# A hybrid decoder layer on one core: two of the weights' four sums by adding transfers, and more chunks with seven products

## The chip, the cores and the metric

One core of a Trainium2 chip. The time is the device time of one launch in microseconds (us). Before the change, three runs took 2104.35, 2105.90 and 2107.91 us; the median is 2105.9.

## What is computed

One decoder layer with 256 tokens, a width of 2048 and a feed-forward width of 5632, all in float32:

```python
def swiglu(x, w_gate, w_up, w_down):
    return (jax.nn.silu(x @ w_gate) * (x @ w_up)) @ w_down

h = h + 0.5 * swiglu(rmsnorm(h, g_ffn1), w1_gate, w1_up, w1_down)
z = rmsnorm(h, g_mix) @ w_in                 # gating MLP and window attention
h = h + concat(rmsnorm(y_a), rmsnorm(y_b)) @ w_out
h = h + cross_attention(rmsnorm(h, g_x), rmsnorm(mem, g_mem), w_xq, w_xkv, w_xo)
h = h + 0.5 * swiglu(rmsnorm(h, g_ffn2), w2_gate, w2_up, w2_down)
out = rmsnorm(h, g_final)
```

The two feed-forwards hold most of the work: two matrices of 2048 x 5632 and one of 5632 x 2048 each.

## The kernel before, in words

**Chunks and units.** Every weight matrix is streamed once, in chunks of 256 rows by two blocks of 512 columns: a tile of [128, 4, 512] float32, 1 MB, whose four rows are called B12, B11, B22 and B21 (slots 0 to 3). A *unit* is all the chunks that add up to the same output columns. In the gate and up part of a feed-forward a unit has 8 chunks (one block of 512 columns of the gate, one of up), and there are 11 units. The down part has 22 chunks and two halves of columns; they are run in four units of 8, 15, 15 and 7 chunks.

**Three matmuls for one product.** A float32 product is made of three passes in fp32r: each operand is split into a high part (a cast, ACT, L148) and a low part (source minus high part, DVE, L149), and high x high, low x high and high x low are summed in PSUM.

**Seven products for eight.** The activations of a chunk are also four blocks (two blocks of 128 tokens by two of 128 rows). A chunk of kind N or C does the 8 block products, 24 matmuls. A chunk of kind S does Strassen's seven (Winograd's form), 21 matmuls; for that it needs four sums of weights, T1 = B11 + B12, T3 = B12 + B22, T2 = T1 + B22 and T4 = T2 + B21, and these have to be split as well. The string KINDS gives the kinds of a unit's 8 chunks, KINDS_D those of the 22 chunks of the down part. C is a kind with 24 matmuls whose activation blocks are combined so that its results fall into the same banks as those of S.

**Loads.** `load` (L298) issues the transfer of a chunk on SP's queue, the split on ACT and DVE, and for S the sums on DVE (L310 two rows at once, L313, L314). There are three buffers for raw chunks, two for high and for low parts, one for the sums (t) and one each for their high and low parts (th, tl). So the transfer of chunk n can start when chunk n-3 has been read by its split and its sums, and chunk n can be split when the matmuls of n-2 have gone through.

**Banks.** PSUM has two pools of four banks. P2, Q3, Q5 and Q4 lie in one (acc). P1, Q7 and Q6, which only S chunks write, lie in the other (trp), from the first S chunk of a unit to the one at index 6; transposes and other side work use what is left of it.

**The end of a unit.** `seven_early` (L479, after chunk 6) copies P1 on ACT and makes v = Q6 - P1 and z = Q7 + v on DVE. `seven_late` (L487, after chunk 7) adds P2, Q5 (twice), Q4 and Q3 to these, which frees the acc banks for the next unit; SiLU on ACT and a product (L585) follow. The 128 x 512 activations so made are transposed on PE (`rows_done`, L565), in two groups of four, a few matmuls into the next unit, and copied by ACT (L575).

**What sets the order.** PE runs in the order of the program. The other engines' instructions, and the transfers that SP and POOL issue, are put in order by a scheduler from priorities and its own costs when the program is built; on the chip each engine takes its own in that order. Chunk 0 and the last chunk of a unit do their products bank by bank (`by_bank`, L349); the others keep the low parts that come last to the end of the chunk.

Of the kernel before, what the change touches and what calls it, by code (L numbers as in the profile page):

```python
# [25 lines left out]
G_FFN1, G_MIX, G_X, G_MEM, G_FFN2, G_Y, B_S = 0, 16, 32, 48, 64, 80, 96  # L26
# [4 lines left out]
def layer_kernel(  # L31
# [22 lines left out]
    nc = tc.nc  # L54
# [3 lines left out]
    stream = ctx.enter_context(tc.tile_pool(name="stream", bufs=2))  # L58
# [9 lines left out]
    def nm(s):  # L68
        uid[0] += 1
        return f"{s}_{uid[0]}"  # L70
# [76 lines left out]
    def split(hi, lo, src):  # L147
        nc.scalar.copy(hi, src)  # L148
        nc.vector.tensor_tensor(lo, src, hi.bitcast(F32), ALU.subtract)  # L149
# [17 lines left out]
    shared = []  # L167
# [84 lines left out]
    def pair_normalized(s, kind, srcT, i, gcol, by_token):  # L252

        raw = s2(s + "r").rearrange("p (k t) -> p k t", k=4)
        src = srcT[i * T:(i + 1) * T, :].rearrange("(k p) t -> p k t", p=P)
        for tb in range(TB):
            a, b = laid(kind, 0, tb), laid(kind, 1, tb)
            nc.gpsimd.dma_start(raw[:, a:b + 1:b - a, :], src[:, :, tb * P:(tb + 1) * P])
        turned = 1 if kind == "S" else 0
        for k in range(2):  # L260
            c = gcol + 2 * i + k
            o = row_tile(kind, raw, k)
            nc.vector.scalar_tensor_tensor(
                out=o, in0=o, scalar=sm[:, c:c + 1], in1=by_token[:, turned:turned + 2, :],
                op0=ALU.mult, op1=ALU.mult,
            )
        p = Pair(s, kind)
        fill(s, p, raw)
        return p
# [28 lines left out]
    def load(s, w, kind, pieces):  # L298

        raw = stream.tile([P, 4, 512], F32, tag="raw", name=nm(s + "w"), bufs=3)  # L300
        wh = stream.tile([P, 4, 512], F32R, tag="wh", name=nm(s + "wh"))
        wl = stream.tile([P, 4, 512], F32R, tag="wl", name=nm(s + "wl"))
        b = {name: (wh[:, i, :], wl[:, i, :]) for name, i in SLOT.items()}
        if kind == "S":
            nc.sync.dma_start(raw, w)
            t = stream.tile([P, 4, 512], F32, tag="t", name=nm(s + "t"), bufs=1)
            th = stream.tile([P, 4, 512], F32R, tag="th", name=nm(s + "th"), bufs=1)
            tl = stream.tile([P, 4, 512], F32R, tag="tl", name=nm(s + "tl"), bufs=1)
            split(wh[:, 1:, :], wl[:, 1:, :], raw[:, 1:, :])
            nc.vector.tensor_tensor(  # L310
                t[:, 0:2, :], raw[:, 1:3, :], raw[:, 0:1, :].to_broadcast([P, 2, 512]), ALU.add
            )
            nc.vector.tensor_tensor(t[:, 2, :], t[:, 0, :], raw[:, 2, :], ALU.add)  # L313
            nc.vector.tensor_tensor(t[:, 3, :], t[:, 2, :], raw[:, 3, :], ALU.add)  # L314
            split(th, tl, t)
            for i, name in enumerate(("T1", "T3", "T2", "T4")):
                b[name] = th[:, i, :], tl[:, i, :]
        elif pieces:
            for i in pieces:
                nc.sync.dma_start(raw[:, i, :], w[:, i, :])  # L320
                split(wh[:, i, :], wl[:, i, :], raw[:, i, :])
        else:
            nc.sync.dma_start(raw, w)
            split(wh, wl, raw)
        return b
# [50 lines left out]
    def side_add(gen):  # L376
        side.append([now[0], gen])
# [62 lines left out]
    def unit(s, w, cb, pairs, beside=None):  # L440

        u = Unit(s, "N" * 8)
        for i in range(8):
            if beside is not None:
                beside(i)
            push(u, i, w[i, cb], lambda i=i: have(pairs, i))
        flush()
        return {(tb, j): u[name] for name, tb, j in BLOCKS}
# [31 lines left out]

# [80 lines left out]
    def ffn(s, get, rs, wgu, wd, on_block, first=None):  # L561
# [36 lines left out]
        def gu_unit(c):  # L598
# [10 lines left out]

            u = Unit(s + "g", KINDS)  # L610
            for i in range(8):
# [159 lines left out]
    n2, on2, rs2_ = next_norm("n2", G_MIX)  # L771
# [2 lines left out]
        first=(n0, prep1, lambda: rs1[0]),  # L774
    )
    mT = []
    partsm = tiny.tile([P, TB, NG], F32, tag="parts", name=nm("parts"))

    def mem_squares(j):
# [34 lines left out]
    by_token = const.tile([P, 3, P], F32, name="by_token")  # L814
# [151 lines left out]
    pu = unit("u", w_in, 0, n2, lambda i: mT.append(pair_normalized("mT", KINDS[i], memT, i, G_MEM, by_token)))  # L966
    with tc.high_priority():
        for name, tb, j in BLOCKS:
            nc.scalar.activation(
# [181 lines left out]
    for cb in range(2):  # L1151
        both = rows_scaled("xq", unit("xq", w_xq, cb, n3), rs3_())
        for j in range(2):
            side_add(attend_memory(2 * cb + j, both[j]))

    n4, on4, rs4_ = next_norm("n4", G_FFN2, KINDS)
    for cb in range(2):
        added_unit("xo", w_xo, cb, xo, on4)
# [114 lines left out]
```

## Time and profile before

| | |
|---|---|
| median of three runs | 2105.9 us |
| profiled execution, and its span | 2105.79 us, 2104.0 us |
| mean granted clock of PE | 0.996 |
| PE, DVE, ACT, POOL busy | 2076.0, 1674.5, 1135.4, 32.2 us |
| read from HBM | 398.52 MB |
| SP's queue q1 | 393.50 MB, 51.7% of 16 engines |
| POOL's queue q0 | 6.30 MB, 0.9% |

A row of a timeline gives start and length in us, engine, line of the kernel, operation, out<-in, and in brackets how long the engine had been idle and what it waited for. A row of a group gives line, engine, operation, shapes and count, then busy time and the mean in ns of one, then idle time of the engine before them and what ended it. In the names, f1g and f2g are the gate and up parts of the two feed-forwards, f1d and f2d the down parts; w, wh, wl are raw chunk, high and low part, t, th, tl the same of the sums; f1gP and f1gQ are the banks.

### The profile page before, as it was taken

Reading aid. Unit: us, or ns where it says so; the run is one execution under the profiler, and the core shown is the slowest. Engines: PE = TensorE matmul, PEld = TensorE weight load, DVE = VectorE, ACT = ScalarE, POOL = GpSimd, SP = SyncE. Lnnn points to the kernel's source line nnn. Section 1 sums busy time; section 2 is a strip of 40 time slices with the busy share of each in tenths; the row PEclk is TensorE's granted clock in tenths of the full one; section 3 lists DMA queues with packets and bytes.
Section 4 is the critical chain, followed back from the end, with each engine's and each line's share of the span. In section 5 each row is a group of like instructions: output and inputs, shape, how many; then the busy total and the mean of one; then the engine's idle time right before and its main releaser. Section 6 shows DMA issues by size and latency. Waiting matters only on the chain.

```text
span 2104.0 us, 23815 instructions
## 1 busy us (share of the span) xinstructions
PE 2076.0 (99%) x9527; PEld 1715.5 (82%) x9527; DVE 1674.5 (80%) x1609; ACT 1135.4 (54%) x1109; POOL 32.2 (2%) x51
## 2 busy tenths in 40 slices
PE   9999999999999999999999999999999999999998
PEld 7888888888888888788888888778888888888886
DVE  5888888888987745867858657798888888889878
ACT  7655555555544645544545455665555545555444
POOL 0000000000000000100000000000000000000000
PEclk9999999999999999999999999999999999999999
DMA  7555555555555554435555543455555555555553
GB/s 281 195 189 213 200 195 184 209 188 199 202 199 206 201 210 166 167 140 200 180 180 184 197 160 140 163 197 200 181 207 197 204 191 200 200 200 200 200 198 122
DMA packets 60110, 402.15 MB, mean 191 GB/s; under 512 B 6864, under 2 KB 8928, under 8 KB 12768
## 3 DMA queue, kind: packets, MB, share of 16 engines
q1 hardware_dynamic: 57280, 393.50, 51.7%
q0 software_dynamic: 2016, 6.30, 0.9%
q8 instruction: 74, 1.21, 0.2%
q10 hardware_dynamic: 704, 0.84, 0.1%
q14 instruction: 36, 0.29, 0.0%
HBM read 398.52 MB, written 2.10 MB: 190 GB/s over the span
## 4 chain that ended last, share of the span: by engine, by line
PE 94%; DVE 3%; ACT 1%; issue 1%; DMA 1%; POOL 0%; SPq 0%; POOLq 0%; DVEq 0%; ACTq 0%
PE f2gQ L363 16%; PE f1gQ L363 15%; PE f1dQ L363 6%; PE f2dQ L363 6%; PE f2gP L363 6%; PE f1gP L363 5%; PE f1dP L363 3%; PE f2dP L363 3%; PE woQ L363 2%; PE xqQ L363 2%; PE f1dR L363 2%; PE f2dR L363 2%; PE xoQ L363 2%; PE mk0Q L363 1%; PE mv1Q L363 1%; PE mv0Q L363 1%
## 5 line engine op out<-in xcount | busy, mean ns | idle before, releaser
L149 DVE TENSOR_TENSOR f1gwl<-f1gw,f1gwh 128x2048 fp32r<-128x2048 f32 (+1 forms) x91 | 185.5, 2043 | 51.6 <-ACT f1gwh L148 51.4
L148 ACT CAST f2gwh<-f2gw 128x1536 fp32r<-128x1536 f32 (+1 forms) x88 | 154.4, 1755 | 133.4 <-PE f2gQ L363 96.6
L148 ACT CAST f1gwh<-f1gw 128x2048 fp32r<-128x2048 f32 (+1 forms) x91 | 156.1, 1716 | 123.5 <-PE f1gQ L363 90.4
L149 DVE TENSOR_TENSOR f2gwl<-f2gw,f2gwh 128x1536 fp32r<-128x1536 f32 (+1 forms) x88 | 183.7, 2088 | 40.3 <-ACT f2gwh L148 40.2
L363 PE MATMUL f2gQ<-f2gwh,n4fh 128*128 128x512 f32 x363 | 141.4, 390 | 0.0
L363 PE MATMUL f2gQ<-f2gwh,n4fl 128*128 128x512 f32 x363 | 141.3, 389 | 0.0
L363 PE MATMUL f1gQ<-f1gwh,n1fh 128*128 128x512 f32 x330 | 128.6, 390 | 0.0
L363 PE MATMUL f1gQ<-f1gwh,n1fl 128*128 128x512 f32 x330 | 128.4, 389 | 0.0
L148 ACT CAST f2dwh<-f2dw 128x2048 fp32r<-128x2048 f32 (+1 forms) x44 | 79.2, 1799 | 91.2 <-PE f2dQ L363 71.2
L148 ACT CAST f1dwh<-f1dw 128x2048 fp32r<-128x2048 f32 (+1 forms) x44 | 79.2, 1799 | 87.9 <-PE f1dQ L363 68.2
L149 DVE TENSOR_TENSOR f2dwl<-f2dw,f2dwh 128x2048 fp32r<-128x2048 f32 (+1 forms) x44 | 94.4, 2145 | 27.0 <-ACT f2dwh L148 24.3
L363 PE MATMUL f2gQ<-f2gwl,n4fh 128*128 128x512 f32 x363 | 115.7, 392 | 0.0
L149 DVE TENSOR_TENSOR f1dwl<-f1dw,f1dwh 128x2048 fp32r<-128x2048 f32 (+1 forms) x44 | 94.3, 2144 | 26.8 <-ACT f1dwh L148 24.2
L363 PE MATMUL f1gQ<-f1gwl,n1fh 128*128 128x512 f32 x330 | 105.1, 392 | 0.0
L149 DVE TENSOR_TENSOR f2gtl<-f2gt,f2gth 128x2048 fp32r<-128x2048 f32 x33 | 75.6, 2292 | 17.0 <-ACT f2gth L148 16.6
L149 DVE TENSOR_TENSOR f1gtl<-f1gt,f1gth 128x2048 fp32r<-128x2048 f32 x30 | 68.8, 2292 | 18.3 <-ACT f1gth L148 18.0
L363 PEld LDWEIGHTS f2gQ<-f2gwh,n4fl 128*128 128x128 f32 x363 | 68.1, 188 | 14.2
L363 PEld LDWEIGHTS f2gQ<-f2gwh,n4fh 128*128 128x128 f32 x363 | 68.2, 188 | 14.1
L363 PEld LDWEIGHTS f2gQ<-f2gwl,n4fh 128*128 128x128 f32 x363 | 67.3, 188 | 13.5
L148 ACT CAST f2gth<-f2gt 128x2048 fp32r<-128x2048 f32 x33 | 63.1, 1913 | 23.1 <-DVE f2gt L314 18.3
L363 PEld LDWEIGHTS f1gQ<-f1gwh,n1fl 128*128 128x128 f32 x330 | 62.0, 188 | 12.9
L363 PEld LDWEIGHTS f1gQ<-f1gwh,n1fh 128*128 128x128 f32 x330 | 62.0, 188 | 12.8
(703 smaller groups left out, 5715.1 us busy)
## 6 DMA issues: line engine op xcount, KB each, us to landing
f2gw<-in_w_gu SPq DMA_DIRECT2D x88, 1024.0 KB, 4.8
f1gw<-in_w_gu SPq DMA_DIRECT2D x87, 1024.0 KB, 4.8
f1dw<-in_w_down SPq DMA_DIRECT2D x44, 1024.0 KB, 4.8
f2dw<-in_w_down SPq DMA_DIRECT2D x44, 1024.0 KB, 4.8
wow<-in_w_out SPq DMA_DIRECT2D x16, 1024.0 KB, 4.8
xqw<-in_w_xq SPq DMA_DIRECT2D x16, 1024.0 KB, 4.8
xow<-in_w_xo SPq DMA_DIRECT2D x16, 1024.0 KB, 4.8
qw<-in_w_in SPq DMA_DIRECT2D x8, 1024.0 KB, 5.0
```

Source lines behind the costliest of these rows:

```text
L148: nc.scalar.copy(hi, src)
L149: nc.vector.tensor_tensor(lo, src, hi.bitcast(F32), ALU.subtract)
L363: nc.tensor.matmul(self.banks[name], x, y, start=name not in self.begun, stop=self.left[name] == 0)
```

## The change

1. `KINDS` goes from CCSCSCSC to SCSCSCSC for the gate and up parts: four of eight chunks are S. The memory's keys and values keep the old string as `KINDS_M`.
2. `KINDS_D` has 8 S in 22 chunks; it had 6.
3. In an S chunk T1 and B12 + B22 are no longer made by DVE. SP loads B11 into slot 0 of the raw tile, B22 into row 0 of t, and slots 1 to 3 as before; POOL then issues two transfers that add B12 to slot 0 (which becomes T1) and to t's row 0 (T3). DVE makes T2 and T4. One split covers all four slots of the raw tile, one the three rows of t. B12 by itself is no longer kept. This holds for all S chunks, in the other stages too. The tile t has three rows and two buffers.
4. `shared.clear()` in two places drops a half-used buffer for the sums of C chunks.

```diff
         if kind == "S":
-            nc.sync.dma_start(raw, w)
-            t = stream.tile([P, 4, 512], F32, tag="t", name=nm(s + "t"), bufs=1)
-            th = stream.tile([P, 4, 512], F32R, tag="th", name=nm(s + "th"), bufs=1)
-            tl = stream.tile([P, 4, 512], F32R, tag="tl", name=nm(s + "tl"), bufs=1)
-            split(wh[:, 1:, :], wl[:, 1:, :], raw[:, 1:, :])
-            nc.vector.tensor_tensor(
-                t[:, 0:2, :], raw[:, 1:3, :], raw[:, 0:1, :].to_broadcast([P, 2, 512]), ALU.add
-            )
-            nc.vector.tensor_tensor(t[:, 2, :], t[:, 0, :], raw[:, 2, :], ALU.add)
-            nc.vector.tensor_tensor(t[:, 3, :], t[:, 2, :], raw[:, 3, :], ALU.add)
+            t = stream.tile([P, 3, 512], F32, tag="t", name=nm(s + "t"))
+            th = stream.tile([P, 3, 512], F32R, tag="th", name=nm(s + "th"), bufs=1)
+            tl = stream.tile([P, 3, 512], F32R, tag="tl", name=nm(s + "tl"), bufs=1)
+            nc.sync.dma_start(raw[:, 0, :], w[:, 1, :])
+            nc.sync.dma_start(t[:, 0, :], w[:, 2, :])
+            nc.sync.dma_start(raw[:, 1:, :], w[:, 1:, :])
+            nc.gpsimd.dma_start(raw[:, 0, :], w[:, 0, :], accum_op=ALU.add)
+            nc.gpsimd.dma_start(t[:, 0, :], w[:, 0, :], accum_op=ALU.add)
+            split(wh, wl, raw)
+            nc.vector.tensor_tensor(t[:, 1, :], raw[:, 0, :], raw[:, 2, :], ALU.add)
+            nc.vector.tensor_tensor(t[:, 2, :], t[:, 1, :], raw[:, 3, :], ALU.add)
             split(th, tl, t)
-            for i, name in enumerate(("T1", "T3", "T2", "T4")):
+            b["T1"] = b.pop("B12")
+            for i, name in enumerate(("T3", "T2", "T4")):
                 b[name] = th[:, i, :], tl[:, i, :]
...
-    KINDS = "CCSCSCSC"
+    KINDS = "SCSCSCSC"
+    KINDS_M = "CCSCSCSC"
...
-    KINDS_D = "NNNNSNSN" + "NNSNSNN" + "NNSNSNN"
+    KINDS_D = "NNSNSNSN" + "NSNSNSN" + "NNSNSNN"
...
-        u = Unit(s, KINDS, sparse=True)
+        u = Unit(s, KINDS_M, sparse=True)
```

**DVE at the joint between two units of the first feed-forward's gate and up part, before.** The first two rows are the low parts of chunk 7 and of the next unit's chunk 0; f1gt_2410 is the sums' tile of that unit's chunk 2; v, p, z and u are the combinations of `seven_early` and `seven_late`.

```order
L149 TENSOR_TENSOR f1gwl_2300<-f1gw_2298,f1gwh_2299 128x2048 [waits DMAHW7_49,PE_49,Activation_49]
L149 TENSOR_TENSOR f1gwl_2333<-f1gw_2331,f1gwh_2332 128x2048 [waits DMAHW0_49,PE_49,Activation_49]
L484 TENSOR_TENSOR f1gv_2326<-f1gQ_377_2173,f1gp_396_2325 128x512 [waits PE_49]
L490 TENSOR_TENSOR f1gp_396_2325<-f1gP_360_2087,f1gp_396_2325 128x512 [waits DVE_49,PE_49]
L485 TENSOR_TENSOR f1gz_2327<-f1gQ_376_2172,f1gv_2326 128x512
L310 TENSOR_TENSOR f1gt_2410<-f1gw_2406 128x1024 [waits DMAHW2_49]
L491 TENSOR_TENSOR f1u_2361<-f1gQ_361_2088,f1gz_2327 128x512 [waits DVE_49,PE_49]
L492 TENSOR_TENSOR f1gv_2326<-f1gQ_361_2088,f1gv_2326 128x512
L494 TENSOR_TENSOR f1gz_2327<-f1gQ_363_2090,f1gz_2327 128x512 [waits DVE_49,PE_49]
L493 TENSOR_TENSOR f1gv_2326<-f1gQ_362_2089,f1gv_2326 128x512 [waits DVE_49]
```

**The same place now.** L315 and L316 are the two sums that DVE still makes, L488 to L498 the lines of `seven_early` and `seven_late`; f1gt_2438 belongs to chunk 0, f1gt_2524 to chunk 2.

```order
L315 TENSOR_TENSOR f1gt_2438<-f1gw_2435 128x512 [waits DMAHW2_49,DMASW2_49]
L316 TENSOR_TENSOR f1gt_2438<-f1gt_2438,f1gw_2435 128x512 [waits DVE_49]
L149 TENSOR_TENSOR f1gwl_2404<-f1gw_2402,f1gwh_2403 128x2048 [waits DMAHW7_49,PE_49,Activation_49]
L149 TENSOR_TENSOR f1gwl_2437<-f1gw_2435,f1gwh_2436 128x2048 [waits PE_49,Activation_49]
L488 TENSOR_TENSOR f1gv_2430<-f1gQ_383_2190,f1gp_414_2429 128x512 [waits PE_49]
L149 TENSOR_TENSOR f1gtl_2440<-f1gt_2438,f1gth_2439 128x1536 [waits DMASW1_49,PE_49,Activation_49]
L494 TENSOR_TENSOR f1gp_414_2429<-f1gP_379_2186,f1gp_414_2429 128x512 [waits DVE_49,PE_49]
L489 TENSOR_TENSOR f1gz_2431<-f1gQ_382_2189,f1gv_2430 128x512
L315 TENSOR_TENSOR f1gt_2524<-f1gw_2521 128x512 [waits DMAHW6_49,DMASW4_49]
L495 TENSOR_TENSOR f1u_2476<-f1gQ_381_2188,f1gz_2431 128x512 [waits DVE_49,PE_49]
L496 TENSOR_TENSOR f1gv_2430<-f1gQ_381_2188,f1gv_2430 128x512
L498 TENSOR_TENSOR f1gz_2431<-f1gQ_384_2191,f1gz_2431 128x512 [waits DVE_49,PE_49]
```

The operation that frees Q3 (L493 before, L497 now) is the next row of the second list. Ahead of it there now stand the low part of chunk 0's sums, and L315, which waits for a POOL transfer (DMASW) where L310 waited for an SP transfer (DMAHW). L315 and L316 of chunk 0 stand ahead of chunk 7's low part.

**PE at the second group of transposes, before** (f1a is the bank that the activations are transposed into; f1gP_375 is P1 of the unit's first S chunk):

```order
L218 MATMUL f1a_2147<-ident,f1gz_2036 128x128
L363 MATMUL f1gQ_361_2088<-f1gwl_2083,n1fh_368 128x512 x2
L363 MATMUL f1gQ_362_2089<-f1gwl_2083,n1fh_331 128x512 x2
L363 MATMUL f1gQ_363_2090<-f1gwl_2083,n1fh_368 128x512 x2
L218 MATMUL f1a_2159<-ident,f1gp_349_2034 128x128
L218 MATMUL f1a_2159<-ident,f1gz_2036 128x128
```

**And now:**

```order
L218 MATMUL f1a_2254<-ident,f1gz_2123 128x128
L366 MATMUL f1gP_378_2185<-f1gwh_2214,n1fh_429 128x512 [waits Activation_49]
L366 MATMUL f1gP_378_2185<-f1gwh_2214,n1fl_430 128x512
L366 MATMUL f1gP_378_2185<-f1gwl_2215,n1fh_429 128x512 [waits DVE_49]
L366 MATMUL f1gP_379_2186<-f1gwh_2214,n1fh_429 128x512
L366 MATMUL f1gP_379_2186<-f1gwh_2214,n1fl_430 128x512
L366 MATMUL f1gP_379_2186<-f1gwl_2215,n1fh_429 128x512
L218 MATMUL f1a_2272<-ident,f1gp_364_2121 128x128 [waits Activation_49]
```

The second group moved from the end of chunk 1 into chunk 2, and it now waits for ACT, which copies the first group out of the one bank that is left.

**POOL's queue now**, for chunks 0, 2 and 4 of the same unit (t's row first, then slot 0 of the raw tile); before it held nothing here:

```order
L313 DMA f1gt_2438<-in_w_gu 128x512 [waits DMAHW0_49,DMASW5_49,DVE_49]
L312 DMA f1gw_2435<-in_w_gu 128x512 [waits DMAHW1_49,DMAHW3_49,DMASW4_49,DVE_49]
L313 DMA f1gt_2524<-in_w_gu 128x512 [waits DMAHW4_49,DMASW0_49,DVE_49]
L312 DMA f1gw_2521<-in_w_gu 128x512 [waits DMAHW5_49,DMAHW2_49,DMAHW7_49,DMASW6_49,DVE_49]
L313 DMA f1gt_2604<-in_w_gu 128x512 [waits DMAHW0_49,DMASW1_49,DVE_49]
```

Each adding transfer waits for SP's plain transfer into the same bytes; SP's queue has three transfers for such a chunk where it had one.

More of the change, by code (lines that the diff above doesn't have):

```diff
@@ L776, in layer_kernel @@
     mT = []
+    shared.clear()
     partsm = tiny.tile([P, TB, NG], F32, tag="parts", name=nm("parts"))
@@ L965, in layer_kernel @@
     ny = [None] * 8
-    pu = unit("u", w_in, 0, n2, lambda i: mT.append(pair_normalized("mT", KINDS[i], memT, i, G_MEM, by_token)))
+    pu = unit("u", w_in, 0, n2, lambda i: mT.append(pair_normalized("mT", KINDS_M[i], memT, i, G_MEM, by_token)))
     with tc.high_priority():
@@ L1154, in layer_kernel @@
             side_add(attend_memory(2 * cb + j, both[j]))
+    shared.clear()
     n4, on4, rs4_ = next_norm("n4", G_FFN2, KINDS)
```

## The prediction

> **What bounds the kernel now.** I read the page first, then a table by stretches, then the timelines of the engines around one joint between two units of a feed-forward, and the transfers last.
>
> ```profile
> PE 2076.0 (99%) x9527; PEld 1715.5 (82%) x9527; DVE 1674.5 (80%) x1609; ACT 1135.4 (54%) x1109; POOL 32.2 (2%) x51
> PE 94%; DVE 3%; ACT 1%; issue 1%; DMA 1%; POOL 0%; SPq 0%; POOLq 0%; DVEq 0%; ACTq 0%
> 226.37:268.81 42.44, 42.44 (x193) 35.14 (x191) 36.21 (x30) 22.50 (x16) 0.00 (x0) 1.00 0.55 197
> ```
>
> The tensor engine is busy throughout and carries 94% of the chain that ended last. The third row is one unit (eight chunks) of the first feed-forward: its columns are length, then busy time of PE, weight load, DVE, ACT and POOL, clock, share of the DMA engines, GB/s. PE has no gap at all in 42.44 us, at full clock; DVE is busy for 36.21. So a product less is time saved, but only while PE is never kept waiting, and DVE has 6 us to spare in 42.
>
> ```profile
> 226.37 0.39 PE L363 MATMUL f1gP<-f1gwh,n1fh 128*128 128x512 f32 x1
> 231.81 0.39 PE L363 MATMUL f1gP<-f1gwh,n1fh 128*128 128x512 f32 x1
> 248.41 0.39 PE L363 MATMUL f1gP<-f1gwh,n1fh 128*128 128x512 f32 x1
> 253.85 0.39 PE L363 MATMUL f1gP<-f1gwh,n1fh 128*128 128x512 f32 x1
> 258.61 0.39 PE L363 MATMUL f1gP<-f1gwh,n1fh 128*128 128x512 f32 x1
> ```
>
> Chunk 7 of a unit begins at 226.37, chunk 0 of the next at 231.81. An ordinary chunk lasts 253.85 - 248.41 = 5.44 us for 24 matmuls, 0.2267 each; one with seven products 258.61 - 253.85 = 4.76 for 21.
>
> **What is saved.** The programs hold 8535 and 8448 matmuls of products: 87 fewer. These are 3 in each of the 21 units with seven products (63), and 2 chunks x 2 halves x 3 in each feed-forward's second matrix (24). 87 x 0.2267 = 19.7 us, all on PE and so on the path: 2105.8 - 19.7 = 2086.1 (the profiled execution took 2105.79 with a span of 2104.0; the median of the runs is 2105.9). The other stages keep their counts, so nothing is saved there.
>
> DVE's work per unit hardly moves: a seven-product chunk loses the sum of two rows (1.22 us), three of its chunks do so, and one more chunk with sums is added. What matters is where that work now stands.
>
> **The joint between two units.** DVE takes its instructions in their order; before, it goes like this.
>
> ```profile
> 221.95 2.29 DVE L149 TENSOR_TENSOR f1gwl<-f1gw,f1gwh 128x2048 fp32r<-128x2048 f32 x1 [2.19 <-ACT f1gwh L148]
> 225.58 2.29 DVE L149 TENSOR_TENSOR f1gwl<-f1gw,f1gwh 128x2048 fp32r<-128x2048 f32 x1 [1.34 <-ACT f1gwh L148]
> 227.78 0.68 DVE L484 TENSOR_TENSOR f1gv<-f1gQ,f1gp 128x512 f32<-128x512 f32 x1
> 228.57 0.69 DVE L490 TENSOR_TENSOR f1gp<-f1gP,f1gp 128x512 f32<-128x512 f32 x1
> 229.18 0.68 DVE L485 TENSOR_TENSOR f1gz<-f1gQ,f1gv 128x512 f32<-128x512 f32 x1
> 229.78 1.22 DVE L310 TENSOR_TENSOR f1gt<-f1gw 128x1024 f32<-128x1024 f32 x1
> 232.71 0.68 DVE L493 TENSOR_TENSOR f1gv<-f1gQ,f1gv 128x512 f32<-128x512 f32 x1
> 254.65 2.28 DVE L149 TENSOR_TENSOR f1gwl<-f1gw,f1gwh 128x2048 fp32r<-128x2048 f32 x1
> 223.63 1.92 ACT L148 CAST f1gwh<-f1gw 128x2048 fp32r<-128x2048 f32 x1 [0.54 <-PE f1gQ L363]
> L149 DVE TENSOR_TENSOR f2gwl<-f2gw,f2gwh 128x1536 fp32r<-128x1536 f32 x33 | 58.0, 1756 | 9.7 <-ACT f2gwh L148 9.7
> ```
>
> (That last row is a group, the 1536-wide subtraction, 1.76 us.) Q3's bank is let go at 232.71 + 0.68 = 233.39. Chunk 0, an ordinary one, asks for it after 12 matmuls, at 231.81 + 2.72 = 234.53: 1.1 us in hand.
>
> Afterwards chunk 0 is a seven-product chunk and asks for Q3 after 6 matmuls: 233.17. And the queue ahead of the release is longer. Its cast cannot start at 223.63, since chunk 6, whose buffer it takes, now reads its first parts until its 11th matmul instead of the 8th (T1 lies among them): +0.68, so 224.31 to 226.23. Then DVE, at the spacing of the rows above: low part 2.2, v 0.6, *the low part of chunk 0's sums* 1.67, P2 0.6, z 0.6, L315 0.6, u, Q5 and Q4 1.8, Q3 0.69, in all 8.76 from 226.3: 235.1. PE waits 235.1 - 233.17, about 2.0 us, even if all data are there.
>
> A second place is the two transposes of the activations. They stood 6 matmuls apart with free banks; now P1, Q7 and Q6 hold three of the four banks from chunk 0 on, and the second needs the first's copy.
>
> ```profile
> 241.12 1.92 ACT L148 CAST f1gwh<-f1gw 128x2048 fp32r<-128x2048 f32 x1 [0.56 <-ACT f1gth L148]
> 242.94 0.58 ACT L575 COPY f1a<-f1a 128x512 f32<-128x512 f32 x1
> L148 ACT CAST f2gwh<-f2gw 128x1536 fp32r<-128x1536 f32 x33 | 49.0, 1485 | 55.8 <-issue 28.7 <-PE f2gQ L363 27.1
> ```
>
> In the new order ACT has the cast, then a 1.49 us cast of the sums, then the copy. Counted from these rows the chunk 3 cast runs to 243.04, the sums to 244.4, the copy to 245.0. PE does its first transposes after chunk 1's 24 matmuls, at 242.69, is through with the next six at 244.5, and waits 0.6.
>
> **The data.** One transfer of 1 MB becomes three on SP's queue and two adding ones on POOL's, each adding one held back until its plain one has landed. L315 needs the one into slot 0 and stands ahead of the four operations that free Q5, Q4 and Q3.
>
> ```profile
> 224.27 0.33 SPq L305 DMA_DIRECT2D f1gw<-in_w_gu  x1
> f1gw<-in_w_gu SPq DMA_DIRECT2D x8, 1024.0 KB, 4.8
> f1gw<-in_w_gu SPq DMA_DIRECT2D x4, 256.0 KB, 4.8
> q1 hardware_dynamic: 1149, 8.36, 55.2%
> L782 POOL DMA_DIRECT2D mr<-in_mem x8: 538/538/606, 714.5 to 737.8; - x8
> DMA to landing us min/median/max: 3.2/4.7/6.2
> ```
>
> The load of chunk 2 starts at 224.27, as soon as chunk 7's low part ends (221.95 + 2.29) and its buffer is free. The last two rows are POOL's own 256 KB loads: 0.54 to issue, 3.2, 4.7 and 6.2 to landing. No row has an adding transfer; these are the nearest, and since it must read what it adds to, I see no way below 3.2. Nor is there a 256 KB load on a quiet SP queue: 8.36 MB in 55.2% of 42.44 us is 357 GB/s, so 768 KB less than the 4.8 us of 1 MB makes 2.6 (an estimate); the four in a crowd took 4.8. With 0.3 for the two hand-overs, the chain from buffer to sum is 6.1 at least (2.6 + 3.2 + 0.3), 7.6 with POOL's median, 9.1 with its longest; the 4.8 would add 2.2 to any of these.
>
> At 6.1 nothing more is lost: 224.27 + 6.1 = 230.4, and DVE reaches L315 only near 232. At 7.6 it is late twice. Chunk 0's own sums stand ahead of chunk 7's low part; their buffer is freed by chunk 5's, which ends at 254.65 + 2.28 - 42.44 = 214.49. So L315 there at 222.1, L316, low part of chunk 7 from 223.3 to 225.6 (not 224.24), chunk 2's data at 233.2, then 3.1 us of DVE to Q3: 236.3. PE waits 3.1. This lateness is passed on, because every seven-product chunk's load is started by a low part that stands behind the sum before it; for that I allow 1.4 more, my choice. So 4.5 + 0.6 = 5.1 per joint. At 9.1 the same steps give 239.3 at Q3 (6.1 waited) and, at chunk 2, the low part of the sums behind L315 of chunk 4: 1.5 more; with 0.6 and 2.8 passed on, 11.
>
> The Trainium skill, "DMA: Bandwidth & Descriptors", section "Anatomy of one DMA", fits a POOL-issued transfer as 2.0 us plus bytes over 436 GB/s, 2.6 us for 256 KB. POOL's rows here, 3.2 at least, do not bear that out under load; by it the chain would be near 5.5 and the sum that of the first rival below. The same skill's "Collectives: The Full Stack", section "The bandwidth ceiling", says a transfer that adds runs at half rate, since it reads two sources. No run here shows it; 0.7 us more per 256 KB would be the result, towards the second rival.
>
> **The sum.** The order has this joint 18 times (nine in each feed-forward): 18 x 5.1 = 92. The other units and 44 seven-product chunks elsewhere load in the same new way; most have no busy joint ahead, so between 0 and 1 us each, 0.3 taken: 13. POOL's own small operations wait behind adding transfers, but the reciprocal roots they make are wanted a chunk or more later: nothing. 2105.8 - 19.7 + 92 + 13 = 2191.
>
> **The rivals.**
> - *Only the queues cost* (0.25): adding transfers land like POOL's fastest loads. 18 x (2.0 + 0.6) = 47 and 5 elsewhere: 2138. For it: DMA engines half idle (0.55 in the unit). It holds while the chain is below about 7 us.
> - *The adding transfers are slow* (0.20), by half rate or by queueing beside 1.25 MB of plain loads: 18 x 11 = 198, with 44 elsewhere: 2328.
> - *Faster* (0.06): PE is not kept waiting, and 2086 results. It needs Q3 to be free at 233.17, two microseconds sooner than DVE's queue allows in my count; for it speak DVE's 6 idle microseconds a unit and two rows less of addition. It decides at a queue of 6.8 us instead of 8.76.
>
> **Numbers.** The forecast has 0.45, the rivals 0.51; 0.04 is left for a wait so small that the time falls between 2095 and 2120. A measurement of this kernel tells 0.2%, 4 us, from no change: faster 0.06, same 0.02, slower 0.92. The low end is 2.0 at each joint and nothing else (2105.8 - 19.7 + 36 = 2122), rounded to 2120; the high end is the slow rival, 2330.
>
> **What would show it.** Right: PE idle at the fourth group of matmuls (Q3) of each unit, released by DVE at the line that subtracts or adds into v, and DVE idle ahead of L315, released by a POOL transfer; units of 46 to 49 us; landing of adding transfers near 4.7. First rival: the same PE gap of 2 us, DVE without idle time before L315, units near 44.4. Second: landings over 6, PE gaps also at the sums' low part in chunk 2, units over 51. Wrong altogether: units of 41.8 with PE busy in all of them.

## The result, and the profile after

The changed kernel takes 2587.95 us (median of 4 runs) where the kernel before takes 2105.91: a ratio of 1.231, 95% interval 1.228 to 1.234. It is 482 us slower. The forecast was 2191, with 2120 to 2330 as the range: the sign was right, the size was not, and the result lies above even the slowest rival (2328).

From the page of the changed kernel: the busy row, the row of the granted clock, and the two queues.

```profile
PE 2198.9 (85%) x9440; PEld 1770.8 (68%) x9440; DVE 1638.6 (63%) x1617; ACT 1176.6 (45%) x1142; POOL 249.0 (10%) x307
PEclk9988889888998999999999999898999888899899
q1 hardware_dynamic: 94144, 427.07, 48.1%
q0 software_dynamic: 38880, 73.43, 16.2%
```

PE did 87 matmuls less and was busy 2198.9 us where it had been busy 2076.0; its share of the span fell from 99% to 85%. The granted clock fell with it, from 0.996 to 0.929 in the mean. So there are two losses, idle time and slow matmuls.

Who waits longest, from the waits of the changed kernel (us in total, times, longest):

```profile
DVE f2gt L315 <- DMA f2gw<-in_w_gu: 255.5, 42, 8.2
DVE f1gt L315 <- DMA f1gw<-in_w_gu: 241.9, 38, 8.8
DVE f1dt L315 <- DMA f1dw<-in_w_down: 66.1, 13, 8.8
PE f2gP L366 <- DVE f2gwl L149: 74.2, 11, 8.1
PE f2gQ L366 <- DVE f2gv L496: 42.3, 9, 5.3
PE f2gQ L366 <- DVE f2gtl L149: 20.1, 9, 2.6
```

DVE waits at L315, the first sum, for nearly every seven-product chunk (42 of 44), 6 us each time; PE then waits for DVE at three places of a unit: for v, behind the first six matmuls of chunk 0 (the place of the forecast), for the low part of the sums, and, the largest, for a plain low part (f2gwl) of the unit's last chunk.

One unit of the second feed-forward on PE's timeline (start, length, operation, in brackets the wait ahead of it):

```profile
2005.47 0.80 PE L366 MATMUL f2gP<-f2gwl,n4fh 128*128 128x512 f32 x1 [7.08 <-DVE f2gwl L149]
2018.79 0.80 PE L366 MATMUL f2gQ<-f2gwh,n4fh 128*128 128x512 f32 x1 [5.04 <-DVE f2gv L496]
2031.73 0.33 PE L218 MATMUL f2a<-ident,f2gp 128*128 128x128 f32 x1 [0.21 <-ACT f2a L579]
2037.40 0.98 PE L366 MATMUL f2gQ<-f2gtl,n4fh 128*128 128x512 f32 x3 [2.23 <-DVE f2gtl L149]
2067.03 0.80 PE L366 MATMUL f2gP<-f2gwl,n4fh 128*128 128x512 f32 x1 [7.76 <-DVE f2gwl L149]
```

From chunk 7 to the next chunk 7 it is 2067.03 - 2005.47 = 61.6 us, and 15.2 of them are waits. The same stretch on DVE shows why:

```profile
2001.79 0.69 DVE L315 TENSOR_TENSOR f2gt<-f2gw 128x512 f32<-128x512 f32 x1 [7.54 <-DMA f2gw<-in_w_gu]
...
2003.13 4.49 DVE L149 TENSOR_TENSOR f2gwl<-f2gw,f2gwh 128x2048 fp32r<-128x2048 f32 x2
...
2010.40 0.68 DVE L489 TENSOR_TENSOR f2gz<-f2gQ,f2gv 128x512 f32<-128x512 f32 x1
2016.84 0.69 DVE L315 TENSOR_TENSOR f2gt<-f2gw 128x512 f32<-128x512 f32 x1 [5.76 <-DMA f2gw<-in_w_gu]
...
2018.05 0.68 DVE L496 TENSOR_TENSOR f2gv<-f2gQ,f2gv 128x512 f32<-128x512 f32 x1
...
2019.25 0.68 DVE L497 TENSOR_TENSOR f2gv<-f2gQ,f2gv 128x512 f32<-128x512 f32 x1
```

At 2001.79 the sum of the next unit's chunk 0 has been waited for. Only behind it comes the low part of chunk 7 (the first of the two at 2003.13), for which PE stood still for 7.08 us. The sum of chunk 2 at 2016.84 stands in the same way ahead of the operations that empty the banks. PE's wait of 5.04 us ended at 2018.79, with L496, which reads Q5's bank, and not with L497, which reads Q3's: that one began at 2019.25, when PE was at work again. So the count ahead of the result, which goes to the end of L497, is two operations (1.2 us) too long.

The chain that feeds that sum, on the queues of SP and POOL:

```profile
2005.44 0.33 SPq L309 DMA_DIRECT2D f2gw<-in_w_gu  x1
2009.76 0.86 POOL L312 DMA_DIRECT2D f2gw<-in_w_gu  x1 [7.65 <-DMA f2gw<-in_w_gu]
```

The plain transfer starts at 2005.44, POOL may issue the adding one at 2009.76, and DVE has the data at 2016.84: 4.3 + 7.1 = 11.4 us, where one transfer of 1 MB had landed after 4.8. The same transfer of the unit's next such chunks starts here:

```profile
2022.16 0.33 SPq L309 DMA_DIRECT2D f2gw<-in_w_gu  x1
2035.70 0.33 SPq L309 DMA_DIRECT2D f2gw<-in_w_gu  x1
2051.74 0.33 SPq L309 DMA_DIRECT2D f2gw<-in_w_gu  x1
2067.00 0.33 SPq L309 DMA_DIRECT2D f2gw<-in_w_gu  x1
```

Each start comes within 0.1 us of the end of a low part that a late sum had held back, and the chain that it begins makes the next sum late: the waits form a ring. From 2005.44 to 2067.00 the four chains took 11.4, 10.6, 12.4 and 11.6 us up to their sums, and DVE's way from each sum through the low part behind it the other 15.5 of 61.6 us. That is the whole unit.

The clock, in stretches of PE (start and end, length, busy time, granted clock, share of the DMA engines, GB/s): after the wait of 5.04 us, later in the unit, and after the wait of 2.23.

```profile
2018.80:2022.40 3.60, 3.60 (x9) 0.50 0.40 71
2025.00:2030.00 5.00, 5.00 (x26) 1.00 0.87 304
2037.40:2041.00 3.60, 3.60 (x16) 1.00 0.88 303
```

After a wait of 5 us PE gets half its clock for 3.6 us; after one of 2.2 us it keeps all of it. The Trainium skill, "TensorE: Matmul & The Clock Gate", Part 1, has the clock halved after a window of some 3.4 us without work and given back after as much work. These rows agree with it (5.04 us of waiting, 3.6 of work). One joint of sum_behind_low, further down, does not: there the clock was halved although no wait was longer than 2.4 us.

By stages (from a stage's first matmul to the next stage's, by the names of PE's banks; us):

| stage | before | after | more |
|---|---|---|---|
| gate/up, first feed-forward | 480.9 | 657.5 | 176.6 |
| down, first | 235.1 | 279.9 | 44.8 |
| attention stages between | 666.2 | 709.1 | 42.9 |
| gate/up, second | 470.2 | 652.8 | 182.6 |
| down, second | 244.9 | 280.6 | 35.7 |

Three quarters lie in the gate/up stages, but the attention stages lost 43 us too, and no kind of chunk was changed there: what they share with the rest is the load.

### The profile page after: what moved, and what is told of

Read it like the earlier page. It is cut to its first block, busy times and chain, and to the rows that moved or that the text cites. A ratio compares the mean times of both kernels' runs of the same rounds, so it can differ in the third digit from the quotient of the medians.

```text
span 2586.7 us, 25145 instructions
## 1 busy us (share of the span) xinstructions
PE 2198.9 (85%) x9440; PEld 1770.8 (68%) x9440; DVE 1638.6 (63%) x1617; ACT 1176.6 (45%) x1142; POOL 249.0 (10%) x307
## 5 line engine op out<-in xcount | busy, mean ns | idle before, releaser
L148 ACT CAST f2gwh<-f2gw 128x2048 fp32r<-128x2048 f32 x88 | 168.1, 1910 | 231.6 <-PE f2gQ L366 131.7
L149 DVE TENSOR_TENSOR f1gwl<-f1gw,f1gwh 128x2048 fp32r<-128x2048 f32 (+1 forms) x91 | 200.1, 2216 | 17.6 <-ACT f1gwh L148 17.5
L149 DVE TENSOR_TENSOR f2gwl<-f2gw,f2gwh 128x2048 fp32r<-128x2048 f32 x88 | 199.4, 2284 | 3.9 <-ACT f2gwh L148 3.9
L315 DVE TENSOR_TENSOR f2gt<-f2gw 128x512 f32<-128x512 f32 x44 | 30.5, 692 | 255.5 <-DMA f2gw<-in_w_gu 255.5
L315 DVE TENSOR_TENSOR f1gt<-f1gw 128x512 f32<-128x512 f32 x40 | 27.7, 692 | 241.9 <-DMA f1gw<-in_w_gu 241.9
L366 PE MATMUL f2gP<-f2gwl,n4fh 128*128 128x512 f32 x176 | 70.0, 428 | 74.2 <-DVE f2gwl L149 74.2
L148 ACT CAST f2dwh<-f2dw 128x2048 fp32r<-128x2048 f32 x44 | 84.0, 1911 | 101.3 <-DMA f2dw<-in_w_down 43.0
L148 ACT CAST f1dwh<-f1dw 128x2048 fp32r<-128x2048 f32 x44 | 83.8, 1910 | 90.1 <-PE f1dQ L366 38.9
L366 PE MATMUL f1gP<-f1gwl,n1fh 128*128 128x512 f32 x160 | 63.7, 428 | 68.7 <-DVE f1gwl L149 68.7
L149 DVE TENSOR_TENSOR f1dwl<-f1dw,f1dwh 128x2048 fp32r<-128x2048 f32 x44 | 100.2, 2286 | 10.9 <-ACT f1dwh L148 8.0
L149 DVE TENSOR_TENSOR f2dwl<-f2dw,f2dwh 128x2048 fp32r<-128x2048 f32 x44 | 100.2, 2286 | 7.6 <-ACT f2dwh L148 7.3
L366 PEld LDWEIGHTS f2gP<-f2gwl,n4fh 128*128 128x128 f32 x176 | 35.3, 201 | 86.3 <-DVE f2gwl L149 79.1
L366 PEld LDWEIGHTS f1gP<-f1gwl,n1fh 128*128 128x128 f32 x160 | 32.1, 201 | 80.1 <-DVE f1gwl L149 73.8
```

What stands on the lines that cost most here:

```text
L315: nc.vector.tensor_tensor(t[:, 1, :], raw[:, 0, :], raw[:, 2, :], ALU.add)
L366: nc.tensor.matmul(self.banks[name], x, y, start=name not in self.begun, stop=self.left[name] == 0)
```

## The experiments

The two kernels differ in three things: the load, the strings of kinds, and by both the order on DVE. **Theory A**: the adding transfers make the way from free buffer to sum (the chain) too long, 11 us against the time that DVE's queue leaves for it (the lead), and DVE, which takes its instructions in order, holds back finished work behind the late sum. **Rivals**: B, the new kinds; C, two transfers in a row whatever they do; D, DVE's order without lateness; E, the extra bytes on SP; F, the rate of the DMA engines; G, waits that only move; H, harm only where chunks with seven products meet at the joint of two units; I, GpSimd's own additions. All times are medians; the kernel before ran beside them at 2105.9 to 2106.3.

| run | kinds | two sums made by | sum behind the low part | time, us | ratio to before (95%) |
|---|---|---|---|---|---|
| before | old | DVE | no | 2105.9 | 1 |
| changed | new | adding transfer | no | 2587.95 | 1.231 (1.228 to 1.234) |
| kinds_only | new | DVE | no | 2209.6 | 1.049 (1.048 to 1.051) |
| load_only | old | adding transfer | no | 2430.2 | 1.155 (1.153 to 1.158) |
| second_plain | new | plain transfer, no sum | no | 2442.3 | 1.160 (1.158 to 1.161) |
| no_second | new | left out | no | 2125.5 | 1.009 (1.008 to 1.011) |
| sum_behind_low | new | adding transfer | yes | 2264.1 | 1.077 (1.075 to 1.079) |
| lead_only | new | adding transfer, longer lead | no | 2202.9 | 1.047 (1.044 to 1.049) |
| order_and_lead | new | adding transfer, longer lead | yes | 2135.6 | 1.015 (1.013 to 1.016) |
| no_second_order | new | left out | yes | 2118.0 | 1.005 (1.004 to 1.007) |
| pool_adds | new | GpSimd | yes | 2170.6 | 1.031 (1.029 to 1.032) |
| load_and_order | old | adding transfer | yes | 2135.6 | 1.015 (1.013 to 1.016) |

### The kinds alone (kinds_only)

The changed kernel with the load of before:

```
-            nc.sync.dma_start(raw[:, 0, :], w[:, 1, :])
-            nc.sync.dma_start(t[:, 0, :], w[:, 2, :])
-            nc.sync.dma_start(raw[:, 1:, :], w[:, 1:, :])
-            nc.gpsimd.dma_start(raw[:, 0, :], w[:, 0, :], accum_op=ALU.add)
-            nc.gpsimd.dma_start(t[:, 0, :], w[:, 0, :], accum_op=ALU.add)
+            nc.sync.dma_start(raw, w)
...
+            nc.vector.tensor_tensor(
+                t[:, 0:2, :], raw[:, 1:3, :], raw[:, 0:1, :].to_broadcast([P, 2, 512]), ALU.add
+            )
...
```

> The changed kernel's strings of kinds (44 more chunks with seven products, 8448 matmuls) with the load of before: one transfer of 1 MB and all four sums on VectorE. Nothing is left out. Theory A (the time went to the chain of the adding transfers: plain transfer landed, issue on GpSimd, adding transfer landed, some 11 us from the buffer coming free to the sum, where it was 4.8): without that chain the 87 matmuls are gained at 0.2267 us, 2105.8 - 19.7 = 2086, and the new joints cost at most what DVE's queue alone makes at the Q3 bank, 2.0 us each at 18 joints: 2086 to 2122, and 2095 as the likeliest. Rival B (the new joints of seven-product chunk after seven-product chunk cost the time, whatever feeds them): close to the changed kernel, above 2350, with PE waiting 5 us or more at chunk 0's Q3 bank in each unit.

2209.6 us: neither. The kinds cost 104 us by themselves, by a way that theory A had not: ten units of the second feed-forward, with columns as in the prediction (length; PE, weight load, DVE, ACT, POOL; clock, DMA share, GB/s).

```profile
1494.10:1956.90 462.80, 434.38 (x1880) 351.54 (x1879) 410.71 (x346) 243.53 (x179) 0.00 (x0) 0.96 0.51 183
```

And, in the same stretch, what PE, DVE and ACT waited for:

```profile
PE f2gQ L363 <- ACT f2gth L148: 18.0, 5, 3.8
...
DVE f2gtl L149 <- ACT f2gth L148: 32.4, 23, 2.1
...
ACT f2gth L148 <- DVE f2gt L314: 58.7, 16, 6.8
```

DVE is busy 41.1 of 46.3 us a unit, and most of the rest goes to waits for ACT, which itself waits for DVE's sums: with all four sums and a fourth such chunk DVE has hardly any room left. With two sums a chunk less on DVE the same kinds take 2125.5 and 2118.0 us (no_second and no_second_order, below). So the new kinds need sums taken off DVE; the question is where to.

### The load alone (load_only)

The kernel before with the changed load, strings of kinds as before.

> The kernel before with the changed load and nothing else: the strings of kinds stay as before (8535 matmuls, 3 seven-product chunks in a gate/up unit, 6 in a down projection), nothing is left out. The other half of kinds_only (2209.6 us). If the chain of the adding transfers costs by itself wherever a seven-product chunk stands (theory A): DVE waits at line 315 for 3 chunks of a unit in place of 4, PE no longer waits for chunk 7's low part, since chunk 0 of the next unit has no sum, and the units go from 42.4 to 48 to 54 us; with some 60 us outside the gate/up stages 2250 to 2450, and 2330 as the likeliest. If the adding transfers hurt only where seven-product chunks meet at the joint (rival H): 2106 to 2150.

2430.2 us, the upper end of theory A's range and far from rival H. The load alone makes 324 of the 482 us, the kinds 104; the 54 that remain need both. PE's longest wait in one unit, and the place on DVE:

```profile
1851.75 0.80 PE L366 MATMUL f2gQ<-f2gwh,n4fh 128*128 128x512 f32 x1 [7.88 <-DVE f2gv L495]
```

```profile
1841.91 0.68 DVE L488 TENSOR_TENSOR f2gz<-f2gQ,f2gv 128x512 f32<-128x512 f32 x1
1849.80 0.69 DVE L315 TENSOR_TENSOR f2gt<-f2gw 128x512 f32<-128x512 f32 x1 [7.21 <-DMA f2gw<-in_w_gu]
```

DVE could empty the banks at 1842.6 and waits 7.2 us for the next unit's sum instead. The joint of before, which nobody had touched, is hit just as hard. Units take (2166.7 - 1627.5) / 10 = 53.9 us. That the low part of chunk 7 causes no long wait here was expected: chunk 0 of the next unit has no sum.

### Adding, or being second? (second_plain, no_second)

Both leave the two additions out: second_plain copies B12 over slot 0 and over row 0 of t where the changed kernel adds it; no_second has no transfers on POOL.

```
-            nc.gpsimd.dma_start(raw[:, 0, :], w[:, 0, :], accum_op=ALU.add)
-            nc.gpsimd.dma_start(t[:, 0, :], w[:, 0, :], accum_op=ALU.add)
+            nc.gpsimd.dma_start(raw[:, 0, :], w[:, 0, :])
+            nc.gpsimd.dma_start(t[:, 0, :], w[:, 0, :])
```

> The changed kernel with its two GpSimd transfers of each seven-product chunk kept but made plain copies: the addition is left out, so slot 0 holds B12 alone. Instructions, waits and bytes to be written stay as they are. Theory A (the length of the chain decides, against a lead of two chunks, 10.4 us, since the sum on line 315 stands ahead of the low part of the chunk before it): the second landing takes 4 to 5 us in place of 7, its issue 0.54 in place of 0.85, so the chain is some 9 us, under the lead; DVE's waits at line 315 shrink from 6 us to 0 to 3 and the time falls to 2120 to 2250. Rival C (two transfers one behind the other in the same buffer cost it, whatever their kind: a wait of SP and POOL on each other): above 2400. Rival B (kinds): above 2350 as well.

> The changed kernel without its two GpSimd transfers: slot 0 holds B11 and row 0 of t holds B22, the two sums are left out. DVE's order, the kinds and SP's three transfers a chunk stay. Theory A: the chain is the plain landing alone, 4 to 5 us against a lead of 10.4: no wait at line 315 to speak of, granted clock of 0.97 or more, 2086 plus at most 2.0 us at 18 joints: 2086 to 2125. Rival D (the order on DVE's queue alone, with the sum at its head): 2138 or more, with PE waiting at the Q3 bank for DVE's own operations. Rival E (SP's three transfers a chunk with 2.0 MB in place of 1 cost it): above 2200.

second_plain: 2442.3 us, not the 2120 to 2250 of theory A; rival C's forecast held. A second transfer that waits for a first one costs 2442.3 - 2125.5 = 317 us even where it only copies, and that it adds costs 146 more. Landings of POOL's transfers, of the changed kernel and of second_plain (issues, size, median us to landing):

```profile
f2gt<-in_w_gu POOLq DMA_DIRECT2D x44, 256.0 KB, 4.2
f2gw<-in_w_gu POOLq DMA_DIRECT2D x44, 256.0 KB, 6.7
```

```profile
f2gt<-in_w_gu POOLq DMA_DIRECT2D x44, 256.0 KB, 3.5
f2gw<-in_w_gu POOLq DMA_DIRECT2D x44, 256.0 KB, 5.7
```

Adding takes 0.7 to 1.0 us more to land, and 0.85 in place of 0.54 to issue. I had taken a plain 256 KB as 4 to 5 us and had the chain fall below the lead of two chunks; the one into slot 0, beside 768 KB of the same chunk, lands after 5.7. In the unit from SP's start at 1857.17 to the one at 1915.06 the four chains still took 9.7 to 10.9 us, and the ring stayed closed.

no_second: 2125.5, at the upper edge of theory A's 2086 to 2125; B, D and E fall, E because SP's three transfers a chunk are all still there (427 MB on its queue). What DVE's order costs on PE when nothing is late:

```profile
PE f2gQ L364 <- DVE f2gv L494: 4.7, 9, 0.5
PE f2a L218 <- ACT f2a L577: 2.1, 10, 0.2
```

0.5 us at the joint and 0.2 at the second transposes; the prediction had counted 2.0 and 0.6.

### The place in DVE's queue (sum_behind_low)

The changed kernel whole; the sums and low parts of a seven-product chunk get an edge that keeps them behind the low part of the chunk before.

```
-            split(wh, wl, raw)
-            nc.vector.tensor_tensor(t[:, 1, :], raw[:, 0, :], raw[:, 2, :], ALU.add)
-            nc.vector.tensor_tensor(t[:, 2, :], t[:, 1, :], raw[:, 3, :], ALU.add)
-            split(th, tl, t)
+            with ExitStack() as behind:
+                if low[0] is not None:
+                    behind.enter_context(tc.issue_after(low[0].ins))
+                low[0] = split(wh, wl, raw)
+                nc.vector.tensor_tensor(t[:, 1, :], raw[:, 0, :], raw[:, 2, :], ALU.add)
+                nc.vector.tensor_tensor(t[:, 2, :], t[:, 1, :], raw[:, 3, :], ALU.add)
+                split(th, tl, t)
...
```

> The changed kernel whole, nothing left out, with one rule of order on VectorE: the sums and the low parts of a seven-product chunk are put behind the low part of the chunk before it, where lines 315 and 316 now stand ahead of it. Theory A: the waiting sum then no longer holds back a low part that is ready, and the lead grows from two chunks to three, 15.7 us against a chain of 11 to 12: DVE still waits at line 315, PE hardly any more; gate/up units of 42 to 46 us in place of 59.5, 2090 to 2200 in all. Rival F (the rate of the adding transfers, 1.56 us of all 16 DMA engines for each, is itself the bound): the DMA share of 0.68 would rise to near 1, units stay above 50 us, above 2400. Rival G (waits merely move to another place in the queue): 2300 to 2600.

2264.1 us: 324 of the 482 come back with the same transfers and the same arithmetic. It is more than theory A's 2200 and less than G's 2300; F falls by its number. What is left on PE:

```profile
PE f2gP L371 <- DVE f2gp L499: 23.1, 10, 2.4
PE f2gQ L371 <- DVE f2gv L501: 7.3, 10, 1.0
PE f2gP L371 <- DVE f2gwl L149: 4.5, 6, 1.4
```

PE's waits for a plain low part (74.2 us in the second gate/up stage) are down to 4.5, and the one shown below is for chunk 0's, no longer chunk 7's; a wait of 2.4 for P2's bank has come at the joint. One joint on PE's timeline, and the clock behind it:

```profile
1811.64 0.50 PE L371 MATMUL f2gP<-f2gwl,n4fh 128*128 128x512 f32 x1 [1.44 <-DVE f2gwl L149]
1814.51 0.50 PE L371 MATMUL f2gP<-f2gwh,n4fh 128*128 128x512 f32 x1 [2.36 <-DVE f2gp L499]
1816.50 0.80 PE L371 MATMUL f2gQ<-f2gwh,n4fh 128*128 128x512 f32 x1 [1.03 <-DVE f2gv L501]
```

```profile
1816.00:1818.00 2.00, 1.50 (x4) 0.50 0.82 317
1820.00:1825.00 5.00, 5.00 (x19) 0.78 0.70 178
```

So no single long wait is needed; 4.8 us in three pieces within 6.3 us halved it too. It came back later than above: the matmuls were slow from 1816.5 to 1822.2, 5.7 us.

### More lead (lead_only, order_and_lead)

The pair of transfers that add gets a tile of its own with two buffers, so that it can start four chunks ahead; the two plain ones into it become one of 512 KB.

```
-            t = stream.tile([P, 3, 512], F32, tag="t", name=nm(s + "t"))
+            t = stream.tile([P, 2, 512], F32, tag="t", name=nm(s + "t"), bufs=1)
+            bs = stream.tile([P, 2, 512], F32, tag="bs", name=nm(s + "s"))
...
-            nc.sync.dma_start(raw[:, 0, :], w[:, 1, :])
-            nc.sync.dma_start(t[:, 0, :], w[:, 2, :])
+            nc.sync.dma_start(bs, w[:, 1:3, :])
             nc.sync.dma_start(raw[:, 1:, :], w[:, 1:, :])
-            nc.gpsimd.dma_start(raw[:, 0, :], w[:, 0, :], accum_op=ALU.add)
-            nc.gpsimd.dma_start(t[:, 0, :], w[:, 0, :], accum_op=ALU.add)
+            nc.gpsimd.dma_start(bs[:, 0, :], w[:, 0, :], accum_op=ALU.add)
+            nc.gpsimd.dma_start(bs[:, 1, :], w[:, 0, :], accum_op=ALU.add)
...
```

Slot 0 and row 0 are then split by themselves, two casts and two low parts more for each such chunk. order_and_lead has the order of sum_behind_low besides, lead_only has not.

> sum_behind_low (2264 us) with more lead besides: slot 0 and row 0 of t become a tile of their own with two buffers, so the pair of transfers that add starts when the seven-product chunk two before it is done with, four chunks ahead in place of three; two more copies and two more low parts a chunk for it, nothing left out. Theory A (the time from buffer to sum decides): the 3.2 us that DVE still waited at the sums of chunk 0 go, the P bank's wait of 2.4 us at the joint with them: 2130 to 2200. Rival F (the DMA engines are the bound; their share was 0.85 to 0.96 in sum_behind_low's units): no gain, 2250 or more.

2135.6 us (theory A: 2130 to 2200). Nearly all the 482 us are back, with every adding transfer still there. Its busy row and POOL's queue:

```profile
PE 2069.2 (97%) x9440; PEld 1698.9 (80%) x9440; DVE 1665.4 (78%) x1873; ACT 1205.4 (57%) x1398; POOL 251.5 (12%) x307
q0 software_dynamic: 38880, 73.43, 20.1%
```

and ten of its gate/up units:

```profile
1452.40:1883.80 431.40, 422.43 (x1886) 344.87 (x1886) 367.21 (x384) 253.17 (x257) 69.39 (x81) 1.00 0.90 269
```

The DMA engines are busy 0.90 of these units, at 269 GB/s, and the units take 43.1 us. The same bytes were moved in 59.5 us units at 0.67 by the changed kernel: the rate was never its bound, and rival F is out. So is rival C as it stands: the two transfers in a row are all still there, and being second cost 317 us only where the sum stood ahead of older work with too little lead. PE's busy time is back at 2069, at a mean clock of 0.992 (0.929 in the changed kernel).

> order_and_lead (2135.6 us) without its rule of order: slot 0 and row 0 of t in a tile of their own with two buffers, the sums on VectorE where the scheduler puts them, nothing left out. It tells which of the two brought the time back from 2588. sum_behind_low (the order alone) gave 2264. If a longer lead is enough, since a sum that is there in time holds nothing back wherever it stands: 2125 to 2180. If the place in the queue matters by itself as well: 2200 to 2400.

2202.9 us: at the lower end of the second range, 2200 to 2400, so the place in the queue matters by itself as well. The lead alone brings back 385 us, the order alone 324, both 452. The larger waits that stay in lead_only:

```profile
PE f2gP L368 <- DVE f2gwl L149: 30.4, 12, 4.4
...
DVE f2gt L317 <- DMA f2gs<-in_w_gu: 64.8, 14, 7.1
```

They are the old pattern, a low part behind a sum that waits, only shorter (30.4 us on PE in place of 74.2).

### The order with nothing late, and with the old kinds (no_second_order, load_and_order)

> no_second (2125.5 us; no transfers on GpSimd, the two sums left out) with the order of sum_behind_low on VectorE. It shows what the order alone is worth when nothing is late. Theory A: the order only removes the sum as a barrier ahead of the low part; with a sum that is never late it gains little, up to the 2.0 us at 18 joints: 2090 to 2125. If the order itself did the good in sum_behind_low in another way than by the lead: below 2090 or above 2130.

2118.0 us, with the sums left out as in no_second: 7.5 less than that, as theory A has it. The order is worth little in itself; what it was worth in sum_behind_low (324 us) is the lateness. It is also the floor of this change here: order_and_lead stands 17.6 us above it, which is what the adding transfers and the extra casts and low parts cost together once the sums are in time.

> load_only (2430.2 us; kinds of before, changed load) with the sums behind the low part of the chunk before them; the first sum of a unit, which stood between lines 488 and 494 of the joint in load_only and kept PE waiting 7.9 us there, then stands behind the joint's operations. Theory A (a late sum at the head of VectorE's queue, not the load as such): the 7.9 us and the lower clock behind it go, units of 43 to 45 us in place of 54, 2115 to 2200, and 2150 as the likeliest. If the load costs by itself (rate of the DMA engines, SP's three transfers): above 2300.

2135.6 us in place of 2430.2: the edge on DVE's queue takes 295 of the 324 us away that the load had cost. DVE still waits for the transfers there, as this row shows, but little that PE needs stands behind the wait (PE's waits for a plain low part are 3.7 us in the second gate/up stage):

```profile
DVE f2gt L320 <- DMA f2gw<-in_w_gu: 53.4, 21, 6.8
```

### The additions on GpSimd (pool_adds)

The order of sum_behind_low, one plain transfer of 1 MB, and GpSimd makes the two sums itself.

```
+            nc.sync.dma_start(raw, w)
+            nc.gpsimd.tensor_tensor(t[:, 0, :], raw[:, 0, :], raw[:, 2, :], ALU.add)
+            nc.gpsimd.tensor_tensor(raw[:, 0, :], raw[:, 0, :], raw[:, 1, :], ALU.add)
...
```

> The changed kernel's kinds and order of sum_behind_low, with the two sums made by GpSimd itself in place of transfers that add: one plain transfer of 1 MB a chunk, two additions of 128x512 on GpSimd, two on VectorE, nothing left out. Theory A (what counts is the time from buffer to sum): one landing of 4.8 us and two additions on an engine that is idle in 99% of the span; if these take 1 to 2 us each the sums are there 7 to 9 us after the buffer came free, inside the lead: 2095 to 2140, a chance to beat the kernel before. Rival I (GpSimd's additions take long, or slow VectorE down while both run): DVE's busy time above 1700 us, 2150 or more.

2170.6 us: rival I's numbers (DVE busy 1757.8 us). An addition took 1.3 to 1.7 us (median), and DVE became slower in the mean; the groups of the sums' low part, without (no_second_order) and with (pool_adds) GpSimd's additions:

```profile
L149 DVE TENSOR_TENSOR f2gtl<-f2gt,f2gth 128x1536 fp32r<-128x1536 f32 x40 | 70.0, 1751 | 0.0
```

```profile
L149 DVE TENSOR_TENSOR f2gtl<-f2gt,f2gth 128x1536 fp32r<-128x1536 f32 x39 | 86.3, 2212 | 0.0
```

The mean hides two cases: of the 44 such low parts of the stage 19 took 2.2 to 2.85 us, and every one of these ran beside an addition on GpSimd; the others, most of them beside one too, took 1.75 as before.

No version tried is faster than the kernel before; with the two sums left out altogether the new kinds still take 0.5% more.

## Why the prediction was right in sign and wrong in size

- **87 matmuls less, -19.7 us: not got.** no_second_order, with the products of the change and nothing late, is 12 us above before, 32 above 2086.1. Two parts of that are located. The start of a feed-forward's gate/up part, from the first matmul to the first z, took 47.1 - 41.5 = 5.6 us (second) and 102.9 - 96.0 = 6.9 us (first, with its plain unit ahead) longer; in the second PE waits 1.2 us for the high and 1.1 for the low part of chunk 0's sums there, and 2.3 for rows that ACT normalizes. And ten units of the second took 42.58 us each, against 42.56 before, although each has 3 matmuls less (0.68 us). With 19 such units these are some 26 of the 32 us. PE idles 0.4 us a unit there (0.1 before), and its busy time fell by 0.3 only; why the runs don't tell.
- **The joint, 2.0 + 0.6 from DVE's and ACT's order alone: too much.** no_second measured 0.5 and 0.2. Of the 2.0, 1.2 are the two operations behind L496 that PE does not wait for: in no_second, too, the operation that reads Q5's bank (L494 there) lets it go.
- **The chain from free buffer to sum, 7.6 us: the term that was mis-sized.** It was 4.3 + 7.1 = 11.4. I took 2.6 us for the plain transfer, an estimate for a quiet queue, and 4.7 for the adding one, the median of POOL's loads in another stage. SP's transfers of one chunk run beside each other, and the small one landed later than it was priced; why is not shown. The prediction's own 4.8 (four 256 KB loads in a crowd) was the better row. The rival of slow transfers had landings over 6 and units over 51: landings of 6.7 (into slot 0; 4.2 into t) and units of 59.5 came, but its 2328 us fell short as well.
- **"Chunk 0's own sums stand ahead of chunk 7's low part": seen, but priced as a delay of DVE only.** I carried it on to Q3's bank and never asked when PE wants chunk 7's low part itself. That wait is the largest on PE: 74.2 and 68.7 us in the two stages. With the 7.6 us of the prediction the low part would have been there at 225.6, ahead of the matmul that takes it; at 11.4 it isn't. The general form was missed: every sum stands ahead of the low part of the chunk before it, so the chain has two chunks of lead (4.76 + 5.44 = 10.2 us), not the three that the three raw buffers suggest. The 4.8 of before fit into that, 11.4 and the sum's own time don't.
- **"For that I allow 1.4 more, my choice": the lateness passed on was the main thing.** It does not die away from chunk to chunk, since the low part that a late sum holds back starts the next chain. Four chains and DVE's work between them set the length of a unit, 61.6 us in the one shown, whatever PE could do; that is why the loss is some 17 us in each of 21 units (59.5 against 42.6 in no_second_order), where the sum had 5.1 at 18 joints. sum_behind_low and load_and_order, which break the ring at the low part, show what it was worth.
- **"Other units and 44 seven-product chunks elsewhere, 13 us": wrong.** load_only has the old kinds everywhere and loses 324 us; the down and attention stages of the changed kernel lose 80 and 43. A sum need not stand at a busy joint to hold back a low part.
- **The clock was not in the sum at all.** Against no_second_order, which has the same products, the changed kernel's span is 2586.7 - 2114.4 = 472 us longer; 2198.9 - 2068.8 = 130 of them are PE's busy time, slower matmuls, and the rest is idle.
- **The weight of the cases.** The rival "slow by half rate or by queueing" was right in kind. second_plain shows the share of its two halves: queueing behind a first transfer 317 us, adding 146. Half rate is close to what the DMA engines show: 1.6 us of all 16 for an adding transfer, 0.86 for the plain copy in its place (worked out below).

Right were the sign, DVE idle ahead of L315 released by a POOL transfer, and PE idle behind chunk 0's first six matmuls, released by v (5.0 us in the unit shown, where 4.5 had been counted; the nearness is chance, since PE was let go 1.2 us sooner than the count has it and the chain was 3.8 us longer).

## What to carry to other kernels

When a load becomes a chain of transfers, count the time from free buffer to last landing, each transfer at its crowded price, and compare it with the lead that the consumer's in-order queue really gives, which is less than the number of buffers says if the waiting operation stands ahead of older work. Then list what is queued behind that operation: here a low part, ready to be made, stood behind a late sum, and one edge of order or a pair of buffers of its own took 324 or 385 of the 482 us back. If the work held back is what frees the next buffer, the lateness goes round in a ring and sets the pace of every unit. A wait of PE of 5 us is dearer than it looks, since the matmuls behind it run at half clock.

## What the runs showed of the hardware that was not expected

- An adding transfer of 256 KB took POOL 0.85 us to issue (0.54 for a plain one) and 6.7 us to land beside the chunk's other transfers (5.7 plain). The queue of the 256 of them took 0.162 x 2586.7 = 419 us of all 16 engines, POOL's other transfers 0.009 x 2123.1 = 19 in no_second: (419 - 19) / 256 = 1.6 us each. For the plain copies of the same bytes in second_plain the same sum gives (0.098 x 2441.0 - 19) / 256 = 0.86.
- In the changed kernel every wait of PE of 3.7 us or more was followed by a lower clock (one half at once after nearly all of them), and none of those of 1.7 to 2.6 us for the sums' low part in the second gate/up stage was; in sum_behind_low three that made 4.8 us within 6.3 halved it too. It came back after some 3.6 us of work, in that last case after 5.7. In the changed kernel that is 130 us, 5% of the span.
- DVE's low part of 1536 columns, 1.75 us alone, took up to 2.85 where GpSimd added at the same time (19 of 44 took 2.2 us or more).
